# How a hybrid decoder layer's first weight transfers are cut and ordered

## The chip, the cores and the metric

The kernel runs on one core of a Trainium2 chip. A core has a matrix engine (TensorE, PE in the profile, with its weight loads as PEld), three engines for elementwise work (VectorE or DVE, ScalarE or ACT, GpSimd or POOL), and SyncE (SP), which here only issues transfers (DMAs) from the chip's memory into the core's on-chip buffer. The engines run side by side and wait for one another by semaphores. The metric is the device time of one execution in microseconds (us); less is better.

## The reference

One decoder layer over 256 tokens of width 1024, in float32:

```
proj  = x @ W_in            # -> q | k | v | B | C | h | gate_attn | gate_conv
y_att = causal attention(rope(q), rope(k), v) @ W_att        # 8 heads of 64
y_cnv = (B * causal_dwconv3(C * h)) @ W_cnv
mix   = (sigmoid(g_att) * y_att + sigmoid(g_cnv) * y_cnv) @ W_o
x     = LayerNorm(alpha * x + mix)
u     = causal_dwconv3(x @ W_up);  f = (silu(u_gate) * u_val) @ W_down
x     = LayerNorm(alpha * x + f)
```

With 256 tokens there is one attention block, so the block selection of the full reference has nothing to choose from. What matters here is the very beginning: q, k and v, each 256 x 512, as products of x (256 x 1024) with the first 1536 columns of W_in. The products are sums over eight slices of 128 of x's 1024 columns.

## The kernel before

**Arithmetic.** To get float32 precision from faster matmuls, each operand is split in a high half (rounded, names ending in h) and a low half (the rest, names ending in l), and a product is made of three matmuls: high by high, high by low and low by high. ScalarE makes the high half by a copy, VectorE the low half by a subtraction (`hl_split`, lines 226 to 228), for the weights as they come and for x.

**Chunks.** The host packs all weights in one array, `wpack`, in the order in which they are used (`plan`, lines 57 to 120). It is read in chunks of up to 128 x 2048 floats. Chunks 0 to 7 hold one slice each: 256 columns of x transposed, then the slice's weights for q (512 columns), k (512) and v (512), 1792 columns in all, which is 896 KB. Later chunks hold 1 MB. A chunk is normally one DMA. `PIECES` (line 52) cuts some into several, at the given columns; `transfers` (lines 123 to 134) lays out the pieces, each contiguous in `wpack`. A reader of a chunk's columns waits only for the pieces that hold them.

**Buffers and the order of the issues.** Chunks go to three buffers (`RAW_BUFS`, line 162) in turn. `issue_dma(c)` (lines 169 to 177) issues every chunk up to c that has not been issued, on SyncE's queue, in the order of the program; a chunk waits there until the buffer that it takes was read for the last time. The schedule is written out by hand: each engine executes its instructions in the order of the code. `issue_dma(1)` (line 235) comes first and issues chunks 0 and 1; at line 265 the small constants follow (`consts`, 128 x 162 floats, 81 KB: convolution taps, gate biases, token positions); then `issue_dma(RAW_BUFS - 1)` at line 596 issues chunk 2. Chunk 3 is issued when chunk 0's buffer is free.

**Beginning.** While the first piece is on its way TensorE does 33 small matmuls on constants (`warm_up`, line 238). Then lines 595 to 608 work through chunk 0 piece by piece: x's high half on ScalarE beside q's high half on VectorE, q's matmuls, the split of k's weights (`split_part`, line 605) and k's matmuls, the split of v's (line 607) and v's matmuls. `qkv_split` (lines 570 to 579) splits the later chunks: x, and then, for chunks 1 and 2, q, k and v one after the other, from chunk 3 on q and k together. The loop from line 611 does for each slice the six matmuls of q, then of k, then of v (line 591), three products for each of two halves of the tokens. Their order in slices 1 to 7 is high by high, then the weights' low half, then x's low half. `rope_tables` (lines 286 to 310) reads the constants first, on VectorE, behind the split of slice 4.

The remaining parts (convolution, gates, attention, output projections, norms, feed-forward) follow with the same split and the same three buffers.

Of the kernel before, what the change touches and what calls it, by code (L numbers as in the profile page):

```python
# [48 lines left out]

CHUNK = 2048  # L50

PIECES = {0: (0, 768, 1280, 1792), 1: (0, 768, 1792)}
OFF_B, OFF_C, OFF_H, OFF_G = 3 * AW, 3 * AW + CW, 3 * AW + 2 * CW, 3 * AW + 3 * CW
TAIL = 8

# [67 lines left out]
def transfers(chunks, units):  # L123

    out, at = [], 0
    for c, us in enumerate(chunks):
        end = units[us[-1]][1] + units[us[-1]][2] * units[us[-1]][3]
        cuts = PIECES.get(c, (0, end))
        assert cuts[-1] == end
# [8 lines left out]
def layer_kernel(ctx: ExitStack, tc: tile.TileContext, x, wpack, cpack, ln1_g, ln1_b, ln2_g, ln2_b, out):  # L138
# [23 lines left out]
    RAW_BUFS, HL_BUFS = 3, 9  # L162
# [6 lines left out]
    def issue_dma(c):  # L169
        while len(raws) <= c and len(raws) < len(chunks):  # L170
            i = len(raws)
            t = wp.tile([P, CHUNK], F32, tag="raw", name=f"raw{i}", bufs=RAW_BUFS)
            raws.append(t)
            for a, b, off in blocks[i]:
                nc.sync.dma_start(t[:, a:b], wpack[off:off + P * (b - a)].rearrange("(p n) -> p n", p=P))
            if i == XR_CHUNK:
                nc.sync.dma_start(xr, x[0].rearrange("(t p) d -> p t d", p=P))
# [84 lines left out]


    consts = cst.tile([P, 162], F32, name="consts")
    nc.sync.dma_start(consts, cpack)
    posi = consts[:, 160:162].bitcast(I32)

# [858 lines left out]
```

## Time and profile before

| What | us |
|---|---|
| median of 3 runs | 363.85 |
| lowest and highest of them | 363.8, 364.34 |
| the profiled execution | 364.61 |
| span of the profiled execution, first to last instruction | 362.8 |

The sizes of the first transfers in order: x with q's weights 384 KB, k's 256 KB, v's 256 KB (chunk 0); x with q's 384 KB, k's with v's 512 KB (chunk 1); the constants 81 KB; chunk 2 with 896 KB. In the profile's list of issues they appear on line 175 (265 for the constants), grouped by size. KB are of 1024 bytes, MB and GB/s decimal.

How to read the rows that follow. A row of the timeline is: start in us, duration in us, engine, line, operation, what is written <- what is read, shapes, and in brackets how long the engine had been idle and what ended that. Neighbouring like instructions are merged (x4 stands for four). `raw` is a chunk's buffer, `wh` and `wl` are the high and low half of weights, `xT` the two halves of x. Line 227 is the helper's high half, line 228 its low half, line 591 the q, k and v matmuls. A row of the chain of waits is a start, a length and the work that everything later waited for. A row of the table by stretches is a stretch of the span, its length, the busy time of each engine, the granted clock of TensorE (PEclk), the share of time in which the DMA engines were busy and what they moved in GB/s.

### The profile page before, as it was taken

To read this page: it belongs to the slowest core of one execution; us is meant where nothing else is said; L and a number is where in the kernel's file an instruction comes from. 1 tells how busy PE (TensorE), PEld (TensorE's weight loads), DVE (VectorE), ACT (ScalarE), POOL (GpSimd) and SP (SyncE) were. 2 spreads that over 40 slices of the span, in tenths; PEclk is the share of its full clock that TensorE was granted. 3 is DMA by queue.
4 is the path that set the end of the run, shared out by engine and by line. 5 is a ranking of instruction groups with operands and counts; after the bars stand their busy time and mean duration, and the time that the engine had idled before them with its cause. 6 is when DMAs were issued, how large, how long until landed. Compare 5 with 4: busy or idle time off the path is not lost.

```text
span 362.8 us, 5271 instructions
## 1 busy us (share of the span) xinstructions
PE 355.3 (98%) x1947; PEld 307.0 (85%) x1947; DVE 299.9 (83%) x518; ACT 235.4 (65%) x431; POOL 24.9 (7%) x48
## 2 busy tenths in 40 slices
PE   8999999999999999999999999999999999999993
PEld 7788888888898888888888888888888888888882
DVE  3787887989795979989769798978869696999795
ACT  4567858787977966653357566675757566588901
POOL 2000001000000113301000000000000000000060
PEclk9999999999999999999999999999999999999998
DMA  7978763626653354687160835447182745653011
GB/s 267 322 267 310 249 225 118 223 116 206 259 191 148 137 221 126 247 323 285 65 233 26 317 122 233 153 194 298 59 341 64 284 129 219 231 234 116 3 58 58
DMA packets 11099, 69.63 MB, mean 192 GB/s; under 512 B 1217, under 2 KB 1473, under 8 KB 4033
## 3 DMA queue, kind: packets, MB, share of 16 engines
q1 hardware_dynamic: 10352, 67.00, 50.4%
q0 software_dynamic: 576, 2.10, 1.7%
q8 instruction: 15, 0.25, 0.3%
q10 hardware_dynamic: 144, 0.20, 0.1%
q14 instruction: 12, 0.09, 0.1%
HBM read 68.24 MB, written 1.05 MB: 191 GB/s over the span
## 4 chain that ended last, share of the span: by engine, by line
PE 92%; issue 2%; DMA 2%; DVE 1%; POOL 1%; SPq 0%; ACT 0%; POOLq 0%; DVEq 0%
PE pb L333 20%; PE pb L340 11%; PE g L333 8%; PE d L315 4%; PE d L316 4%; PE d L317 4%; PE g L340 4%; PE y L333 4%; PE q L591 3%; PE v L591 3%; PE k L591 3%; PE b L333 2%; PE y L340 2%; PE c L333 2%; PE h L333 2%; PE o L316 2%
## 5 line engine op out<-in xcount | busy, mean ns | idle before, releaser
L205 DVE TENSOR_TENSOR wl<-raw,wh 128x1024 fp32r<-128x1024 f32 x99 | 122.1, 1235 | 23.3 <-ACT wh L196 22.7
L196 ACT ACTIVATE wh<-raw 128x1024 fp32r<-128x1024 f32 x99 | 103.7, 1054 | 26.9 <-DMA raw<-in_wpack 26.7
L333 PE MATMUL pb<-x1T,wh 128*128 128x512 f32 x320 | 76.2, 390 | 0.0
L333 PEld LDWEIGHTS pb<-x1T,wh 128*128 128x128 f32 x320 | 59.7, 188 | 12.1
L340 PEld LDWEIGHTS pb<-x1T,wl 128*128 128x128 f32 x320 | 41.0, 191 | 1.6
L340 PE MATMUL pb<-x1T,wl 128*128 128x256 f32 x320 | 41.5, 283 | 0.0
L228 DVE TENSOR_TENSOR wl<-raw,wh 128x1024 fp32r<-128x1024 f32 (+1 forms) x29 | 27.3, 982 | 7.2 <-ACT wh L227 7.0
L333 PE MATMUL g<-xT,wh 128*128 128x512 f32 x128 | 31.8, 395 | 0.0
L315 PE MATMUL d<-wh,f 128*128 128x512 f32 x80 | 31.3, 391 | 0.0
L316 PE MATMUL d<-wl,f 128*128 128x512 f32 x80 | 31.3, 391 | 0.0
L317 PE MATMUL d<-wh,f 128*128 128x512 f32 x80 | 31.1, 389 | 0.0
L227 ACT ACTIVATE wh<-raw 128x1024 fp32r<-128x1024 f32 (+1 forms) x29 | 23.7, 859 | 9.0 <-DMA raw<-in_wpack 5.1
L333 PEld LDWEIGHTS g<-xT,wh 128*128 128x128 f32 x128 | 23.2, 188 | 4.6
L858 ACT ACTIVATE fb<-pb 128x512 f32<-128x512 f32 x20 | 11.9, 596 | 16.8 <-PE pb L340 16.8
L876 DVE SCALAR_TENSOR_TENSOR fc<-fb,consts,fc 128x254 f32<-128x254 f32 x40 | 19.4, 484 | 1.4
L874 DVE SCALAR_TENSOR_TENSOR fc<-fb,consts,fc 128x255 f32<-128x255 f32 x40 | 19.1, 478 | 0.0
L868 ACT ACTIVATE fc<-fb,consts 128x256 f32<-128x256 f32 x40 | 18.0, 497 | 0.4 <-DVE fb L862 0.4
L317 PEld LDWEIGHTS d<-wh,f 128*128 128x128 f32 x80 | 15.0, 188 | 3.2
L1024 POOL TENSOR_TENSOR fs<-fs 128x512 f32<-128x512 f32 (+2 forms) x5 | 5.8, 1163 | 169.7 <-ACT fs L1021 169.5
L315 PEld LDWEIGHTS d<-wh,f 128*128 128x128 f32 x80 | 15.1, 189 | 2.7
L316 PEld LDWEIGHTS d<-wl,f 128*128 128x128 f32 x80 | 15.1, 189 | 2.6
L340 PEld LDWEIGHTS g<-xT,wl 128*128 128x128 f32 x128 | 16.4, 191 | 0.7
(207 smaller groups left out, 613.4 us busy)
## 6 DMA issues: line engine op xcount, KB each, us to landing
raw<-in_wpack SPq DMA_DIRECT2D x55, 1024.0 KB, 5.0
raw<-in_wpack SPq DMA_DIRECT2D x6, 896.0 KB, 6.8
xr<-in_x SPq DMA_DIRECT2D x1, 1024.0 KB, 7.0
ln<-in_ln_g POOLq DMA_DIRECT2D x2, 512.0 KB, 5.5
ln<-in_ln_b POOLq DMA_DIRECT2D x2, 512.0 KB, 6.1
raw<-in_wpack SPq DMA_DIRECT2D x2, 384.0 KB, 4.5
raw<-in_wpack SPq DMA_DIRECT2D x2, 256.0 KB, 4.3
raw<-in_wpack SPq DMA_DIRECT2D x1, 512.0 KB, 6.9
```

The source lines that it names most:

```text
L196: nc.scalar.activation(units[u]["h"], raw_of(u), AF.Copy)
L205: nc.vector.tensor_tensor(units[u]["l"], raw_of(u), units[u]["h"].bitcast(F32), op=ALU.subtract)
L227: nc.scalar.activation(h, src, AF.Copy)
L228: (eng or nc.vector).tensor_tensor(l, src, h.bitcast(F32), op=ALU.subtract)
L315: nc.tensor.matmul(o, ah, bh, start=start, stop=False)
L316: nc.tensor.matmul(o, ah, bl, start=False, stop=False)
L317: nc.tensor.matmul(o, al, bh, start=False, stop=stop)
L333: nc.tensor.matmul(bank, un["h"][:, k, n0:n0 + P], b[:, k].rearrange("p a s -> p (a s)"), start=k == 0, stop=False)
L340: nc.tensor.matmul(bank[:, 0:S], un["l"][:, k, n0:n0 + P], b[:, k, 0], start=False, stop=k == nk - 1)
L591: nc.tensor.matmul(banks[m][t], (xl if p == 2 else xh)[:, k, t * P:(t + 1) * P], wl if p == 1 else wh, start=k == 0 and p == 0, stop=k == ...
L874: nc.vector.scalar_tensor_tensor(c[:, 1:S], pb[:, a * S:a * S + S - 1], w_ffn(1, j), c[:, 1:S], op0=ALU.mult, op1=ALU.add)
L876: nc.vector.scalar_tensor_tensor(c[:, 2:S], pb[:, a * S:a * S + S - 2], w_ffn(0, j), c[:, 2:S], op0=ALU.mult, op1=ALU.add)
```

## The change

Chunk 0 comes in two pieces in place of three: x with q's weights as before (columns 0 to 768), then k's with v's (768 to 1792). Chunk 1 comes in one piece in place of two. Chunk 2 is issued ahead of the constants. SyncE has two issues fewer, and the order of its queue is now chunk 0 (384 KB, 512 KB), chunk 1 (896 KB), chunk 2 (896 KB), constants, chunk 3 and so on. The instructions of the other engines and their order are the same; the host's layout of `wpack` follows the pieces. From line 265 on the changed kernel's lines have numbers one higher.

```diff
-PIECES = {0: (0, 768, 1280, 1792), 1: (0, 768, 1792)}
+PIECES = {0: (0, 768, 1792)}
...
     consts = cst.tile([P, 162], F32, name="consts")
+    issue_dma(RAW_BUFS - 1)
     nc.sync.dma_start(consts, cpack)
```

The `issue_dma(RAW_BUFS - 1)` of line 596 stays and finds nothing left to issue.

## The prediction

> **What bounds the kernel now.** I read the busy line of the page first, then busy time in chosen stretches of the span.
>
> ```profile
> span 362.8 us, 5271 instructions
> PE 355.3 (98%) x1947; PEld 307.0 (85%) x1947; DVE 299.9 (83%) x518; ACT 235.4 (65%) x431; POOL 24.9 (7%) x48
> ```
>
> ```profile
> core 0: us, PE busy (x) PEld busy (x) DVE busy (x) ACT busy (x) POOL busy (x), PEclk, DMA share, GB/s
> 4.40:9.90 5.50, 5.15 (x20) 3.22 (x19) 3.25 (x6) 2.61 (x5) 0.00 (x0) 1.00 0.99 361
> 9.90:351.00 341.10, 341.08 (x1851) 294.86 (x1852) 288.37 (x489) 229.51 (x420) 21.71 (x28) 1.00 0.53 193
> ```
>
> TensorE is the bound, and without a gap: from 9.90 to 351 it is busy 341.08 of 341.10 us. Nothing after 9.90 can take up a delay, and nothing there can be sped up by an earlier load. So the change is worth exactly what it does to the moment at which that unbroken run of matmuls begins. The chain of waits, cut to the first 13 us, says what sets this moment.
>
> ```profile
> 2.12 6.06 DMA raw<-in_wpack
> 8.18 0.02 issue
> 8.20 0.42 ACT xT L227
> 8.62 0.53 ACT wh L227
> ...
> 9.17 0.70 DVE wl L228
> 9.87 0.04 issue
> 9.92 1.41 PE q L591 x5
> 11.33 1.36 PE k L591 x6
> ```
>
> The run begins at 9.92, with the second q matmul of chunk 1 (it needs the low half wl). Backwards: wl is made at 9.17, after wh at 8.62, after x at 8.20, after a landing at 8.18: the fourth transfer, x and q's weights of chunk 1. So **landing + 1.74 us = TensorE's start** (9.92 less 8.18). Six matmuls last 1.36 us, 0.227 each.
>
> Next the timeline, for all landings that somebody waits for, and for TensorE behind them.
>
> ```profile
> 3.71 0.42 ACT L598 ACTIVATE xT<-raw 128x256 fp32r<-128x256 f32 x1 [1.68 <-DMA raw<-in_wpack]
> 4.28 1.25 PE L591 MATMUL q<-wh,xT 128*128 128x512 f32 x4
> 4.48 0.63 ACT L227 ACTIVATE wh<-raw 128x512 fp32r<-128x512 f32 x1 [0.35 <-DMA raw<-in_wpack]
> 5.38 0.62 PE L591 MATMUL q<-wl,xT 128*128 128x512 f32 x2
> 5.84 0.62 PE L591 MATMUL k<-wh,xT 128*128 128x512 f32 x2
> 6.96 0.63 ACT L227 ACTIVATE wh<-raw 128x512 fp32r<-128x512 f32 x1 [1.85 <-DMA raw<-in_wpack]
> 7.64 0.73 PE L591 MATMUL v<-wh,xT 128*128 128x512 f32 x2 [0.27 <-ACT wh L227]
> 8.37 0.50 PE L591 MATMUL v<-wl,xT 128*128 128x512 f32 x1
> 9.49 0.63 ACT L227 ACTIVATE wh<-raw 128x512 fp32r<-128x512 f32 x1 [0.35 <-DMA raw<-in_wpack]
> ```
>
> ScalarE stood idle ahead of each of the ACT rows until a DMA came, so their starts are the landings: x and q of chunk 0 at 3.71, k at 4.48, v at 6.96, k and v of chunk 1 at 9.49 (x and q of chunk 1 at 8.18, above). A weight that lands at time T feeds its high half to TensorE at T + 0.68 (7.64 less 6.96) and its low half at T + 1.41 (8.37 less 6.96).
>
> **The change part by part.** Bytes, engines' instructions and their order stay as they are; only SyncE's list changes.
>
> *x and q of chunk 0:* still the first transfer, the same 384 KB. Landing 3.71, first q matmul 4.28: nothing.
>
> *k with v of chunk 0.* The k weights lost a landing of their own at 4.48 and now come with v. Call that landing K. At the same bytes as now it is v's, 6.96. TensorE has finished q at about 5.84 and then waits: two k matmuls from K + 0.68, the third from K + 1.41, three more, then all six of v without a wait (ScalarE splits v straight behind k, 0.63 us; VectorE takes 0.69 for each low half, so v's is there by K + 2.1, before it is needed). After its third, k has four starts of 0.227 to go, so v begins at K + 2.32, and chunk 1 at K + 3.68; its second matmul could go at **K + 3.91**. With 6.96 that is 10.87 against 9.92: 0.95 late.
>
> *Chunk 1 in one transfer.* x and q can only be split when k and v are there too. Call this landing L. At the same bytes as now L is 9.49, where the last piece of chunk 1 lands today. The chain from landing to the second q matmul is the same four steps, so TensorE starts at **L + 1.74**. With 9.49 that is 11.23: 1.31 late. It lies behind K + 3.91, so L decides, and the k wait hides wholly beside it; the two do not add. K would decide only above L − 2.17. The new waiting instruction is ScalarE's x copy; behind it in ScalarE's line are the three weight copies of chunk 1, and VectorE and TensorE wait for all of them. After it k and v of chunk 1 are no longer waited for: their copies of 0.63 follow one another, and their low halves of 0.69 each come before the 6 × 0.227 = 1.36 of matmuls in front of them have run.
>
> *What a landing costs* is the open price: the trace shows no transfer of these sizes behind that first one. Both ends come from these stretches.
>
> ```profile
> 2.00:3.50 1.50, 1.50 (x17) 1.50 (x15) 0.00 (x0) 0.03 (x1) 0.62 (x12) 1.00 0.96 343
> 3.50:5.50 2.00, 2.00 (x14) 1.71 (x13) 1.76 (x4) 1.05 (x2) 0.00 (x0) 1.00 0.85 240
> 5.50:6.50 1.00, 1.00 (x6) 0.82 (x5) 0.34 (x1) 0.00 (x0) 0.00 (x0) 1.00 0.96 319
> 6.50:9.50 3.00, 2.73 (x11) 1.53 (x9) 1.45 (x3) 1.58 (x4) 0.00 (x0) 1.00 1.01 405
> ```
>
> The last column is what the DMA engines moved, in GB/s. From 3.71 on, 512 KB (k, v) and 896 KB (chunk 1), 1.442 MB, have to come. At 405 GB/s throughout they would take 3.56 us: K = 5.00, L = 7.27, and a start at 9.01, 0.91 **earlier** than now. At 240 throughout they would take 6.01: L = 9.72, a start at 11.46, 1.54 later. The ends for this term are −0.91 and +1.54. I take it close to 9.49, the one row in which these very bytes, in this order, have landed; since fewer, larger transfers can hardly make the stream worse and may take some of the slow stretch away, I move it a tenth of the way to 7.27, to L = 9.27. That is a choice, not a reading. Start 11.01, **+1.09 us**.
>
> The Trainium skill speaks for the change here: "DMA: Bandwidth & Descriptors", section Bandwidth, advises batching transfers to 1 MiB or more, and its fit has about 2 us of fixed cost for each. By that, an estimate, one transfer less in chunk 1 would bring L to about 7.5 and the start to 0.7 earlier; the trace so far disagrees, since 512 KB landed 1.31 us behind the piece before it, less than one fixed cost. It is taken up as the first rival.
>
> *Chunk 2 ahead of the constants.*
>
> ```profile
> 0.74 2.28 SPq L175 DMA_DIRECT2D raw<-in_wpack  x5
> 3.07 0.43 SPq L265 DMA_DIRECT2D consts<-in_cpack  x1
> 11.88 0.42 ACT L227 ACTIVATE xT<-raw 128x256 fp32r<-128x256 f32 x1 [1.24 <-DMA raw<-in_wpack]
> 12.86 1.90 DVE L228 TENSOR_TENSOR wl<-raw,wh 128x512 fp32r<-128x512 f32 x3
> 14.12 0.39 PE L591 MATMUL q<-wl,xT 128*128 128x512 f32 x1
> 21.57 0.16 DVE L300 CAST posf<-consts 128x2 f32<-128x2 int32 x1
> ```
>
> Five issues took 2.28 us, 0.46 each. Chunk 2 moves from the seventh issue (after the constants' 0.43 at 3.07) to the fourth, at about 2.1; the constants become the fifth. All this is issued long before the queue gets to it, so only the order counts: chunk 2 has 81 KB less ahead, 0.2 us at 405 GB/s. It lands at 11.88 now, its first low half is ready at 12.86 + 0.63 = 13.49, and TensorE takes it at 14.12: 0.63 us of slack, and 1.7 once TensorE starts 1.09 later. Worth nothing. The constants come behind 896 KB more, some 2.3 us later, near 12, and their first reader, VectorE at 21.57, hides that; without this cover it would stop VectorE's line, where the low halves are. Chunk 3 waits for chunk 0's buffer, which is free when v's low half is made: 7.62 + 0.69 now, at most K + 2.1 = 9.06 after, below 0.8 later.
>
> ```profile
> 7.62 0.69 DVE L228 TENSOR_TENSOR wl<-raw,wh 128x512 fp32r<-128x512 f32 x1 [1.78 <-ACT wh L227]
> 14.58 0.42 ACT L227 ACTIVATE xT<-raw 128x256 fp32r<-128x256 f32 x1 [0.71 <-DMA raw<-in_wpack]
> 18.20 0.39 PE L591 MATMUL q<-wl,xT 128*128 128x512 f32 x1
> ```
>
> Chunk 3's copy starts at 14.58 and its low half is used at 18.20, itself 1.09 later: 3.6 us for a chain of under 3. Nothing.
>
> **Sum.** 0 + 0 (hidden) + 1.09 + 0 + 0. The profiled execution took 364.61, 1.8 around its span of 362.8; with 1.09 it would be 365.70. The runs shown have a median of 363.85, 0.76 below the profiled one; I carry the difference over: 363.85 + 1.09 = **364.95 us**. About 0.2%, 0.73 us, is what a measurement of this kernel tells from no change.
>
> **Rivals.**
> *1. The stream runs smoother (faster).* Mechanism: the 240 GB/s of 3.50 to 5.50 is made by the small transfers, and two larger ones run at 405. For it: the slow stretch lies just where the two 256 KB pieces are under way. Against it: 343 GB/s before, over the first, 384 KB. It decides below L = 8.18: there landing + 1.74 is under 9.92. At L = 7.4 the start is 9.14, 0.78 earlier: **363.07**. Chunk 2's slack of 0.63, plus the 0.2, carries that.
> *2. Part of it.* The merged chunk gains about what waiting for its last piece costs: L from 7.9 to 8.9. At 8.4 the start is 10.14, 0.22 later: **364.07**.
> *3. The clock falls.* In the forecast TensorE waits between 5.84 and about 7.6, and again before 11.01.
>
> ```profile
> 0.78 3.68 PE L241 MATMUL warm<-const-bfloat16-1.0 128*128 128x128 bf16 x33 [0.78 <-PEq L1116]
> 355.00:358.80 3.80, 1.49 (x13) 1.28 (x11) 2.94 (x9) 0.95 (x4) 0.66 (x1) 1.00 0.00 0
> 358.80:362.80 4.00, 0.00 (x0) 0.00 (x0) 0.87 (x2) 0.00 (x0) 0.00 (x0) 0.58 0.35 131
> ```
>
> At the end, TensorE is busy only 1.49 of the 3.80 us from 355.00 and idle afterwards; the granted clock is still 1.00 in that stretch and 0.58 in the next. So more than 2.3 us of idleness was borne at full clock, and the forecast's longest wait is 1.8. If the clock fell all the same, a half-speed stretch as long as the 3.68 us of warming matmuls would cost 1.84: **366.8**. The Trainium skill, "TensorE: Matmul & The Clock Gate", Part 1, puts the fall after one idle window of about 3.4 us; the trace's last rows agree.
>
> **How the numbers follow.** Forecast (L from 8.9 to 9.72, +0.72 to +1.54): 0.60. Rival 1 (L below 7.9): 0.16, half of it past 0.73. Rival 2: 0.20. Rival 3: 0.04. Faster 0.08, same 0.28, slower 0.64. The range takes in the bounds −0.91 and +1.54 on 363.85, 362.9 to 365.4, cut a little below, as rival 1's end holds little, and 0.3 wider above for the spread of the runs shown (363.8 to 364.34): 363.1 to 365.7.
>
> **What would show it.** In the profile after: ScalarE's second copy starts at K, not at 4.48, and its first x copy of chunk 1 at L; TensorE's second q matmul of chunk 1 at L + 1.74, near 11.0, and no gap behind it; no DMA wait of VectorE at the constants. It would be wrong if L came before 8.2, if K lay above L − 2.17, or if TensorE showed a gap later on or a clock below 1.00.

## The result, and the profile after

The changed kernel takes 365.4 us (median of 6 runs, 364.69 to 365.47), the kernel before 364.19 (also 6 runs). The ratio is 1.0032, with a 95% interval of 1.0022 to 1.0042: **slower by about 1.2 us**. Forecast was 1.09 slower.

The trace taken with these runs is of the fastest of the six, 364.69, and it does not show the forecast's wait. Its timeline on ScalarE (start, duration, line, operation, and what ended the idle time before):

```profile
3.97 0.42 ACT L599 ACTIVATE xT<-raw 128x256 fp32r<-128x256 f32 x1 [1.95 <-DMA raw<-in_wpack]
5.20 1.15 ACT L227 ACTIVATE wh<-raw 128x512 fp32r<-128x512 f32 x2 [0.82 <-DMA raw<-in_wpack]
7.89 0.42 ACT L227 ACTIVATE xT<-raw 128x256 fp32r<-128x256 f32 x1 [1.54 <-DMA raw<-in_wpack]
```

k and v land together at 5.20 (K), the whole of chunk 1 at 7.89 (L): both early. In the chain of waits of the same trace, over the first 14 us, there is no transfer at all:

```profile
...
0.78 3.68 PE warm L241 x33
4.46 0.09 issue
4.54 2.61 PE q L592 x6
7.15 1.39 PE k L592 x6
8.54 1.37 PE v L592 x6
9.91 1.36 PE q L592 x6
...
```

The first six q matmuls took 2.61 us, the next six 1.36: TensorE was the bound from its first real matmul, because it ran at about half speed until some 6.7 us. Its second q matmul of chunk 1 came at 9.97, against 9.92 before.

A median is explained by a usual execution, not by the fastest. So the same kernel was traced again (the run e7_after_again, below). This execution took 365.62, a little above the median; the two traces lie on either side of it. The second one's chain of waits:

```profile
...
1.64 7.38 DMA raw<-in_wpack
9.02 0.02 issue
9.04 0.42 ACT xT L227
9.46 0.53 ACT wh L227
9.99 0.02 issue
10.01 0.70 DVE wl L228
10.72 0.04 issue
10.76 1.44 PE q L592 x5
...
```

This is the chain shown of before with one landing exchanged for another: the whole of chunk 1 at 9.02 in place of x and q's weights at 8.18; then the same four steps, and TensorE at 10.76, which is 9.02 + 1.74. Behind it nothing changed, as the busy times by stretches say for the repeated run (341.00 busy of 341.00 us):

```profile
core 0: us, PE busy (x) PEld busy (x) DVE busy (x) ACT busy (x) POOL busy (x), PEclk, DMA share, GB/s
10.90:351.90 341.00, 341.00 (x1851) 294.77 (x1852) 288.13 (x489) 228.64 (x419) 21.71 (x28) 1.00 0.52 191
```

So an execution's time is the moment of the second q matmul of chunk 1 plus a constant: 364.61 less 9.92 is 354.69 before, 364.69 less 9.97 is 354.72 in the first trace after, 365.62 less 10.76 is 354.86 in the second. In all eleven traces of this document the difference lies between 354.57 and 354.86. The usual 365.4 then stands for a start near 10.6, and, if that start is a landing plus 1.74, for a landing near 8.9. This is worked out, not read: no execution of exactly that time was traced.

### The profile page after: what moved, and what is told of

It is laid out like the page before. It is cut to its first block, busy times and chain, and to the rows that moved or that the text cites. A ratio compares the mean times of both kernels' runs of the same rounds, so it can differ in the third digit from the quotient of the medians.

```text
span 362.9 us, 5266 instructions
## 1 busy us (share of the span) xinstructions
PE 355.6 (98%) x1947; PEld 307.9 (85%) x1947; DVE 299.5 (83%) x518; ACT 235.2 (65%) x431; POOL 25.4 (7%) x48
## 4 chain that ended last, share of the span: by engine, by line
PE 95%; issue 2%; DVE 1%; POOL 1%; POOLq 0%; DVEq 0%
PE pb L334 20%; PE pb L341 11%; PE g L334 8%; PE d L316 4%; PE d L317 4%; PE d L318 4%; PE g L341 4%; PE y L334 4%; PE q L592 3%; PE k L592 3%; PE v L592 3%; PE b L334 2%; PE y L341 2%; PE c L334 2%; PE h L334 2%; PE o L317 2%
```

## The experiments

Theory A is the prediction's: TensorE begins its unbroken run 1.74 us behind the landing of the last piece of chunk 1 that the first splits need. Theory B, the rival which the first trace suggests: the pieces matter little, and the start is set by when TensorE's clock is released. Theory C: what costs is the k weights' lost landing of their own.

**e1_chunk0_two: chunk 0 in two transfers, nothing else.**

```diff
-PIECES = {0: (0, 768, 1280, 1792), 1: (0, 768, 1792)}
+PIECES = {0: (0, 768, 1792), 1: (0, 768, 1792)}
```

> Chunk 0 in two transfers, chunk 1 in its two as before, constants ahead of chunk 2 as before. Theory A (the last piece of chunk 1 sets TensorE's start; k's wait hides beside it): x and q of chunk 1 still land by themselves, so TensorE starts at their landing + 1.74, as before: within 0.4 us of the kernel before. Theory B (the transfers' sizes do little; the start is set by when TensorE's clock is released, which differs from execution to execution): within 0.4 us too, and so are the other kernels of this call. Theory C (the k weights' lost landing costs): 0.9 to 1.2 us slower.

Measured: 364.02 against 364.18, ratio 1.0 (0.9988 to 1.0012). Theory C's 0.9 to 1.2 us lie far outside the interval, whose upper end is 0.44 us: theory C falls, and a landing of their own for the k weights shows no worth in this kernel.

**e2_chunk1_one: chunk 1 in one transfer, nothing else.**

```diff
-PIECES = {0: (0, 768, 1280, 1792), 1: (0, 768, 1792)}
+PIECES = {0: (0, 768, 1280, 1792)}
```

> Chunk 1 alone in one transfer, chunk 0 in three and the constants ahead of chunk 2 as before. Theory A: the whole loss of the changed kernel, 1.0 to 1.3 us slower than before, with TensorE's second q matmul of chunk 1 1.74 us behind the landing of the merged chunk. Theory B: within 0.4 us of before. Theory C: within 0.4 us of before.

Measured: 365.43 against 364.18, ratio 1.0036 (1.0022 to 1.0049). This one cut accounts for the whole loss; theory B falls as the explanation of the difference. The trace, of the fastest of its 12 runs (364.63), has TensorE waiting for chunk 1 all the same:

```profile
...
8.15 0.02 issue
8.18 0.42 ACT xT L227
...
9.89 1.42 PE q L591 x5
```

From the landing at 8.15 to the matmul at 9.89 it is 1.74 once more.

**e3_order_only: chunk 2 ahead of the constants, all pieces as before.**

```diff
     consts = cst.tile([P, 162], F32, name="consts")
+    issue_dma(RAW_BUFS - 1)
     nc.sync.dma_start(consts, cpack)
```

> All pieces as before, chunk 2 issued ahead of the constants. Theories A, B and C: within 0.3 us of before. If chunk 2 or the constants carried a cost or a gain, it would show here.

Measured: 364.33 against 364.18, ratio 1.0001 (0.9986 to 1.0015). No cost or gain of the order shows; the interval leaves room for 0.55 us at most.

**e4_cut_at_v: the changed kernel, chunk 1 cut ahead of v.**

```diff
-PIECES = {0: (0, 768, 1792)}
+PIECES = {0: (0, 768, 1792), 1: (0, 1280, 1792)}
```

> The changed kernel, but chunk 1 is cut ahead of v: x, q and k in one transfer of 640 KB, v in one of 256 KB. Theory A: the wait is shorter by what 256 KB take, 0.63 us at 405 GB/s, so about half of the changed kernel's loss: 0.4 to 0.7 us slower than before. Theory B: within 0.4 us of before, by chance. Theory C: as the changed kernel, 1.2 us slower.

Measured: 364.69 against 364.18, ratio 1.0011 (0.9999 to 1.0023): between. The median is inside theory A's span, though the interval alone doesn't rule out no change. The trace (364.81) has the 640 KB piece landing at 8.30 and the matmul at 10.04, 1.74 later:

```profile
...
8.30 0.02 issue
8.32 0.42 ACT xT L227
...
10.04 1.43 PE q L592 x5
```

With x and q alone, with k, with k and v in the piece that the first split waits for, the ratios are 1.0001 (e3), 1.0011 (e4) and 1.0032 (the changed kernel). Their order is the one of theory A, the cost growing with what has to land first, though the interval of each touches the next one's.

**e5_after_short_chain and e6_before_short_chain: the 1.74 itself.** The chain behind the landing of chunk 1 is made as short as chunk 0's, in the changed kernel and in the one before.

```diff
-    qkv_split(1)
+    issue_dma(RAW_BUFS)
+    split_start(4)
+    nc.scalar.activation(xh[:, 1, :], raws[1][:, 0:S], AF.Copy)
+    nc.vector.tensor_copy(units[4]["h"][:, 0], raw_of(4)[:, 0])
+    nc.vector.tensor_tensor(xl[:, 1, :], raws[1][:, 0:S], xh[:, 1, :].bitcast(F32), op=ALU.subtract)
+    nc.vector.tensor_tensor(units[4]["l"][:, 0], raw_of(4)[:, 0], units[4]["h"][:, 0].bitcast(F32), op=ALU.subtract)
+    split_part(4, 1, 2)
+    split(5)
...
-            qkv_passes(k, m, (0, 1), (0, 1, 2))
+            if k == 1 and m == 0:
+                for p in (0, 2, 1):
+                    qkv_passes(1, 0, (0, 1), (p,))
+            else:
+                qkv_passes(k, m, (0, 1), (0, 1, 2))
```

> The changed kernel, with the chain from chunk 1's landing to TensorE made shorter as it is for chunk 0: VectorE copies q's high half while ScalarE copies x's, and q's matmuls go in the order high by high, x's low half, weights' low half, so that four of them run ahead of the weights' low half. From landing L, that half is ready at L + 1.6 (0.43 + 0.43 + 0.69 and starts), and is needed by the fifth matmul in place of the second: a start equal to L + 0.92 in place of L + 1.74. Theory A (the merged landing plus its chain is what TensorE waits for): 0.6 to 0.85 us faster than the changed kernel, 364.6 to 364.8, about 0.5 slower than before. Theory B (clock release): no change, 365.2 to 365.6. Theory C (k's wait): no change either.

Measured: 364.41, where the changed kernel, measured beside it, took 365.3 and the kernel before 364.28; ratio to before 1.0 (0.9989 to 1.0012). That is 0.9 us less than the changed kernel, where 0.6 to 0.85 was expected, and a median a little below the span given. Nothing but the work behind chunk 1's landing was changed, so that work was what TensorE waited for. In the trace the next thing is late now, the k weights:

```profile
...
5.66 0.64 ACT wh L227
...
6.35 1.92 PE k L592 x6
8.27 1.37 PE v L592 x6
9.64 1.36 PE q L592 x6
```

> The kernel before, with the same shorter chain. Theory A: TensorE waits for x and q of chunk 1 here too, at an earlier landing; at most 0.82 faster, less where the matmuls of chunk 0 or v's landing then decide: 363.4 to 363.9, faster than both kernels. Theory B: no change, 364.0 to 364.4.

Measured: 363.99 against 364.28, ratio 0.9991 (0.9982 to 1.0). It is clearly faster than the changed kernel, but only just apart from the one before, and the gain is short of what was expected. Compared like with like, both with the short chain, the merged pieces still cost 0.42 us: 364.41 (e5) against 363.99, and eight of e5's 11 runs are above the slowest of e6's. So e5 is level with the kernel before because the short chain is worth more where the landing is later; the cost of the pieces is not gone. The trace of e6 says what sets its start instead: the chain has no transfer, only TensorE, whose first six q matmuls took 2.16 us.

```profile
...
0.78 3.68 PE warm L241 x33
4.46 2.16 PE q L591 x6
6.62 1.37 PE k L591 x6
...
9.36 1.36 PE q L591 x6
```

**e7_after_again: the changed kernel, traced once more.** No edit.

> The changed kernel once more, for a second trace: the first trace's execution took 364.69, the other five 365.4. Theory A: the usual execution has chunk 1 landing near 8.9 to 9.3, TensorE's second q matmul of chunk 1 1.74 behind it (10.6 to 11.0), and a release of the clock that does not decide. Theory B: the usual execution has an early landing (below 8) and a late release of the clock.

Measured: 365.3 (364.06 to 365.72) against 364.28, ratio 1.0023 (1.0011 to 1.0034). The trace is the one shown above: landing at 9.02, start at 10.76, as theory A has it. TensorE had been done with v and idle for 0.69 us when the first q matmul could go:

```profile
8.96 0.39 PE L592 MATMUL v<-wl,xT 128*128 128x512 f32 x1
...
9.04 0.42 ACT L227 ACTIVATE xT<-raw 128x256 fp32r<-128x256 f32 x1 [2.80 <-DMA raw<-in_wpack]
...
10.04 0.51 PE L592 MATMUL q<-wh,xT 128*128 128x512 f32 x1 [0.69 <-ACT wh L227]
...
10.76 0.51 PE L592 MATMUL q<-wl,xT 128*128 128x512 f32 x1 [0.22 <-DVE wl L228]
```

**e8_two_and_two_short: e1's cut with e6's shorter chain.**

```diff
 # on top of e6
-PIECES = {0: (0, 768, 1280, 1792), 1: (0, 768, 1792)}
+PIECES = {0: (0, 768, 1792), 1: (0, 768, 1792)}
```

> The kernel before with chunk 0 in two transfers (chunk 1 stays in its two) and with the shorter chain for chunk 1. Theory A: both landings that TensorE can wait for are early or hidden, so that mostly the matmuls of chunk 0 themselves set the start: 363.5 to 363.9, 0.3 to 0.7 faster than before, and about as fast as the shorter chain alone. If it is not faster than the shorter chain alone, the cut of chunk 0 carries nothing.

Measured: 364.06 against 364.14, ratio 1.0005 (0.9992 to 1.0019): a miss, not faster. Ten of its 12 runs are at 363.81 to 364.72, two at 365.4 and 365.45, and the trace is of the slowest. In it the k weights, now tied to v's, landed at 6.76:

```profile
...
6.76 0.02 issue
...
7.47 1.92 PE k L591 x6
9.39 1.37 PE v L591 x6
10.76 1.36 PE q L591 x6
```

The second q matmul came at 10.82, where K + 3.91 gives 10.67. So k's tie to v is free only behind something later: in this execution, with x and q of chunk 1 there and split in time, k and v landed late and set the start. The other slow execution was not traced.

**e9_after_no_warm_up: the changed kernel with one warming matmul.**

```diff
-    warm_up(33)
+    warm_up(1)
```

> The changed kernel with 1 warming matmul in place of 33, so that TensorE begins chunk 0 at half speed and stays so for 3 to 6 us. The matmuls up to the second q of chunk 1 (19) would take up to 0.43 each in place of 0.227: 8 us at most from 4.3, a start between 10.5 and 12.4. Theory A (the landing plus 1.74, near 10.7, decides in the changed kernel): 0 to 1.7 slower than the changed kernel, about 0.7, since the wait for the landing takes up a part. Theory B (the clock decides throughout): 2 us slower or more.

Measured: 365.91 against 364.14, ratio 1.005 (1.0032 to 1.0068); about 0.55 above the changed kernel's 365.3 and 365.4, which were measured at other times. Twelve matmuls ran at half speed:

```profile
...
4.49 2.90 PE q L592 x6
7.38 2.54 PE k L592 x6
9.92 1.40 PE v L592 x6
11.32 1.37 PE q L592 x6
```

They cost 2.72 us more than 1.36 for each six would have, and 0.55 of it reached the end. The trace of e7 shows where most of the rest lay. There the first six q matmuls took 2.00 (from 4.44 to k's first at 6.44), so 0.64 was lost to slow matmuls already, and TensorE stood idle for 1.35 in all ahead of its second q matmul of chunk 1 (10.76, where it would have come at 9.41 without the waits). So the clock is the second bound of this stretch, close behind the landing, and not the cause of the difference.

## Why the prediction was right

**The bound.** TensorE without a gap after its start, and the change worth the shift of that start: right, in every trace (no idle time from 11.60 to 351 in the traces of e1 to e6, e8 and e9 either).

**Landing + 1.74.** Right to the hundredth in e2, e4 and e7, whose landings differ by 0.87 us. e5 shows from the other side that it is this chain. It holds only where the landing is what TensorE waits for: the prediction named L before 8.2 as a sign of being wrong, and in the first trace L was 7.87 and the start 0.36 later than L + 1.74.

**Which landing decides.** Right: L and not K (e1 and e2). K itself was far off, 5.18 and 5.06 in the changed kernel's two traces where 6.96 was taken, so that the forecast wait for the k weights was not there to hide. K + 3.91 was 0.15 short as well: in the traces in which k decided it was 4.06 (e5: 5.64 to 9.70; e8: 6.76 to 10.82). **Nothing for chunk 2 and the constants:** right within e3's interval; VectorE's first reader of the constants doesn't wait in the changed kernel, either.

**The size.** 1.09 forecast, 1.2 measured. The time itself, 364.95 forecast and 365.4 measured, is off mostly because the kernel before has a median of 364.19 over more runs, not 363.85.

**The mis-sized step is the landing's level.** The prediction took L from one execution: 9.49, moved to 9.27. Measured are 7.87 and 9.02 (ScalarE begins 0.02 later). The 9.49 and the 8.18 of the trace before both belong to an execution above the median (364.61). Had the usual 364.19 also been a landing plus 1.74, x and q would usually land near 7.8, and the whole chunk near 8.9 in place of 9.27: both levels too late by about 0.4. That they were off by the same is not something that the prediction argued, so the closeness of 1.09 to 1.2 is in part luck. The other traces bear the size out roughly: chunk 1 in one transfer landed at 7.87, 8.15, 8.42, 8.47 and 9.02 (the two traces after, e2, e5, e9), x and q of chunk 1 alone at 6.77, 6.92, 7.73, 8.08 and 8.18 (before, e1, e3, e6, e8), on average 0.85 earlier.

That L could be read from a mean rate failed too. The stream did become smoother, as the first rival has it; here are GB/s (last column) from 3.50 to 6.50 in the changed kernel's two traces:

```profile
3.50:5.50 2.00, 1.92 (x11) 1.52 (x10) 1.45 (x3) 0.71 (x2) 0.00 (x0) 1.00 1.03 421
5.50:6.50 1.00, 1.00 (x4) 0.77 (x3) 0.64 (x2) 0.85 (x2) 0.00 (x0) 1.00 1.02 423
```

```profile
3.50:5.50 2.00, 2.00 (x12) 1.58 (x11) 1.45 (x3) 0.83 (x2) 0.00 (x0) 1.00 1.00 411
5.50:6.50 1.00, 1.00 (x6) 0.82 (x5) 0.75 (x2) 0.74 (x2) 0.00 (x0) 1.00 1.01 401
```

It was 240 and 319 before. With 401 to 411 in the second trace, the 1.442 MB behind the first landing (3.87) would have been in at about 7.4; the landing was 9.02. The trace's completion records, one for each of the 16 DMA engines of a transfer, tell why: eight of the sixteen had finished chunk 1 by 7.16, fifteen by 7.49, the last one at 9.02 (8th and last: 7.10 and 7.87 in the first trace; 6.45 and 8.18 for x and q of chunk 1 before). A landing is its slowest engine's. The Trainium skill, "DMA: Bandwidth & Descriptors", section Why a DMA increments its semaphore by 16 and not by 1, says that the engines of a transfer finish independently and that only the full count means that all data is there; these records agree. What holds an engine up by up to 1.9 us is open: no run here separates it. The smoother stream itself goes with the two merged transfers taken together: the four traces with both have 401 to 434 GB/s from 3.50 to 5.50 (after, e5, e7, e9), the other seven 240 to 352, e2 with chunk 1 alone merged 342 and e1 with chunk 0 alone 316. Behind 5.50 the two groups are not apart.

**The rivals.** Smoother transfers, faster: the mechanism was there, the gain was not, because the landing is the slowest engine's and not the mean's. It decided one traced execution of two, and there half-speed matmuls had taken the bound over: L + 1.74 would have been 9.61, TensorE came at 9.97. The price that the prediction drew from the Trainium skill does not apply: "DMA: Bandwidth & Descriptors", section Anatomy of one DMA — SWDGE (gpsimd) path, gives the fit with about 2 us for transfers on GpSimd's path, and here SyncE issues; e2, with that one transfer less, landed at 8.15 in its trace and not at the 7.5 of that estimate.

The clock did not fall through the waits: it stays at 1.00 behind them in the repeated run too (the stretch from 10.90 above). The longest wait there was 0.69, not the forecast's 1.8; but in e8's trace TensorE stood idle for about 1.7 (5.78 to 7.47), and the clock was 1.00 behind that too. The argument against this rival was weaker than it looked all the same. That 2.3 us of idleness are borne at full clock, read from one trace, is no safe bound: at the end of e2 TensorE has nothing to do from 356.50 on, and the clock has already fallen at 358.44, after 1.94 us:

```profile
356.50:358.40 1.90, 0.00 (x0) 0.00 (x0) 1.40 (x5) 0.00 (x0) 0.67 (x1) 1.00 0.00 0
358.50:362.80 4.30, 0.00 (x0) 0.00 (x0) 1.17 (x2) 0.00 (x0) 0.00 (x0) 0.50 0.33 122
```

In the kernel before it fell after 2.95 us, and in the changed kernel's first trace only after 5.21. So the 3.4 us that the prediction took from the Trainium skill, "TensorE: Matmul & The Clock Gate", Part 1, agree with these ends only as a middle value.

## What to carry to other kernels

Cut a transfer behind what its first reader needs: in a starting pipeline the bound engine can wait for a landing plus the chain behind it, and a merged transfer puts the last byte in front of the first use. A mean rate doesn't give a landing, and a single traced execution gives one draw of it: trace the usual execution before explaining a median. Where a landing can't come earlier, shorten the chain behind it; here that took back 0.9 us, though with the same short chain the smaller pieces were still 0.4 us ahead.

## What the runs showed of the hardware

TensorE's half speed at the beginning ends at a different moment in each execution, with the same 33 warming matmuls ahead: the first four q matmuls took 1.25 us before, 1.69 in e7 and 2.05 in the first trace after.

```profile
4.54 2.05 PE L592 MATMUL q<-wh,xT 128*128 128x512 f32 x4
```

```profile
4.44 1.69 PE L592 MATMUL q<-wh,xT 128*128 128x512 f32 x4
```

The column of the granted clock has 1.00 over all of that time (the rows above from 3.50 on). The trace's first record of the clock, however, begins only at the release: at 4.46 before, 5.59 in e7 and 6.67 in the first trace after. In that last trace the second to fifth q matmuls start 0.43 apart, and those from 6.75 on 0.23. In the ten traces with 33 warming matmuls the release lies between 3.45 and 6.67. The Trainium skill, "TensorE: Matmul & The Clock Gate", Part 1, says that the window which decides is free-running, so that the transition depends on where in it the first matmul falls. The records agree: the stretch at full clock lasts 354.99 us in nine of the eleven traces, 358.40 in e8 and 351.57 in e9, so the lengths differ by steps of 3.41, and the spread of the ten releases, 3.22, is within one step. The moment of the release bounds what an earlier landing can still bring here: in e6 and in the first trace after, TensorE's own slow matmuls were the whole chain.
